# Down products and their way back to the tokens from one set of four PSUM banks

## The chip, the cores and the metric

The kernel runs on one core of a Trainium2 chip. The metric is the device time of one execution in microseconds (us). The kernel before took 1285.71 us, the median of three runs (1284.75 to 1287.04). One more execution was profiled; it took 1283.96 us, of which 1282.1 us lie between the first and the last instruction (the span).

Engines: TensorE (PE, with its weight loads as PEld) multiplies into PSUM, which has eight banks of 512 float32 for each of 128 partitions. VectorE (DVE) and ScalarE (ACT) read PSUM; GpSimd (POOL) works on SBUF alone; SyncE (SP) issues the loads of weights.

## The reference

Two layers, each an attention mixer and a mixture of experts, over 512 tokens of width 1024 in float32. The change lies in the mixture of experts: each token goes to two of 32 experts, each an MLP with a hidden width of 256.

```python
def hierarchical_moe(h, ...):
    ...                      # comb: each token's weight for its 2 of 32 experts, else 0
    y = jnp.zeros_like(hf)
    for g in range(N_GROUPS):
        a = jnp.einsum('nd,edf->nef', hf, w_gate[g])
        u = jnp.einsum('nd,edf->nef', hf, w_up[g])
        y = y + jnp.einsum('nef,efd->nd', jax.nn.silu(a) * u * comb[:, g, :, None], w_down[g])
    return y.reshape(B, S, D)

def reference(...):
    for l in range(DEPTH):
        ...
        x = x + gate_m * hybrid_mixer(h, ...)
        h = rms_norm(x, norm_ffn[l]) * (1.0 + scale_f) + shift_f
        x = x + gate_f * hierarchical_moe(h, ...)
    return x
```

## The kernel before

Each expert gets 64 slots for tokens. The expert stage (`moe`) goes through the experts in pairs, in 16 iterations a layer, so that the two experts of a pair fill the 128 partitions. One iteration `i` has these parts, in TensorE's order:

1. `down(i-1)` (lines 1062 to 1090): two tiles `d`, one for each half `q` of the 1024 output columns, 8 matmuls each. VectorE scales each with the slot weights and the gate (L1082, `o`), ScalarE and GpSimd split that into `ohi` and `olo` (L1087, L1088).
2. `hidden(i)` (lines 1035 to 1051): 32 matmuls into one tile `gu`; then the silu on ScalarE (L1049) and the product on VectorE (L1050) give `hs`.
3. The combine of pair `i-1`, from iteration 1 to 14: eight units, one for each of four token tiles `tt` and two halves `q`. A unit (`combine`, lines 1112 to 1118) is two matmuls with a 0/1 matrix `oT` that brings the rows of the slots back to their tokens, into a tile `y`; then `add` (L1095) on VectorE adds the tile to the residual stream `x`. Behind every second unit stands a pair of transposes `g` that gather rows for a later iteration (L1022), whose results VectorE and ScalarE copy out as `gT` (L1028, L1030). Behind the sixth unit stands the turn of `hs` (L1057), which ScalarE copies out as `hT` (L1059): the input of the next `down`.

Iteration 14 has nothing left to gather; iteration 15 has no combine, and `combine_last` (lines 1120 to 1140) does pairs 14 and 15 together, its first five units in five banks at once.

PSUM tiles come from `bank(name, tag, bufs)` (line 61). Tiles with one tag share `bufs` banks; a new tile waits until a bank of its tag has been read out. In the expert stage the tags are `d` (2), `y` (2), `g` (2), `gu` (1) and `misc` (1), all eight banks. `pm` (line 76) keeps the matmuls of the stage in the order in which they are written; the transposes are kept too. The instructions of VectorE and ScalarE around them are ordered when the program is built.

Weights come by DMA from SyncE's queue: 2 MB of gate and up weights (`wgu`, five tiles) and 1 MB of down weights (`wd`, four tiles) for each expert. Experts `2i+5` and `2i+6` are loaded into the tiles that `hidden(i)` frees, experts `2i+4` and `2i+5` of the down weights into those that `down(i)` frees. The gathered rows come by indirect DMA from GpSimd (L1003).

Of the kernel before, what the change touches and what calls it, by code (L numbers as in the profile page):

```python
# [29 lines left out]
def hybrid_decoder_kernel(ctx, tc, x, c, w_ada, b_ada, norm_mix, norm_ffn, w_in, w_gk2, b_gk, q_gain,  # L30
# [30 lines left out]
    def bank(name, tag, bufs, shape=None):  # L61
        return psum[1].tile(shape or [P, 512], F, name=name, tag=tag, bufs=bufs)
# [10 lines left out]
    def mm(o, a, b, start, stop):  # L73
        T.matmul(o, a, b, start=start, stop=stop, skip_group_check=True)  # L74

    def pm(o, a, b, start, stop):

        tc.keep_in_program_order(T.matmul(o, a, b, start=start, stop=stop, skip_group_check=True))  # L78

    def keep_warm(b, n):  # L80

        ps = bank("warm", "y", 2)
        for _ in range(n):
            pm(ps[:, 0:b.shape[-1]], ident, b, True, True)

# [799 lines left out]
    def moe(l, xt, ss, pool):  # L885
# [79 lines left out]
        for k, ix in ((0, i1), (1, i2)):  # L965
# [5 lines left out]
        V.tensor_tensor(exn.rearrange("p (t k) e -> p t (k e)", k=2), ex.rearrange("p t k e -> p t (k e)"),  # L971
                        tok[:, :, None].to_broadcast([P, NT, 2 * NE]), op=OP.mult)
        keep_warm(lo.rearrange("p t e -> p (t e)"), 10)

        rk = misc("rk", [P, NT + 1, NE])
        for tt in range(NT + 1):
            for t2 in range(min(tt + 1, NT)):
                pm(rk[:, tt], after_b if t2 == tt else ones_b, both[:, t2], tt == 0, t2 == min(tt, NT - 1))
        keep_warm(lo.rearrange("p t e -> p (t e)"), 6)
        pos = t3(2, "pos")  # L980
        tmp = pool.tile([P, NT, 2, NE], F, name="tmp")
# [80 lines left out]
        def down(hT, ws, i=None):  # L1062

            n = len(ws)
            r = slice(0, 64 * n)
            parts, last = [], None
            if i == NE // 2 - 1:

                last = wgu([P, 2, 2, 512], R, name="last")
            for q in range(2):  # L1070
                pd = bank("d", "d", 2)
                for j in range(2):
                    for e in range(n):
                        pm(pd[64 * e:64 * e + 64], hT[:, j, 64 * e:64 * e + 64],
                           ws[e][:, D * j + 512 * q:D * j + 512 * q + 512], j == 0, j == 1)
                o = ot([P, 512], name="o")
                gate = gates[l, 5][r, 512 * q:512 * q + 512]
                if i is None:
                    V.tensor_tensor(o[r], pd[r], gate, op=OP.mult)
                    parts.append(o)  # L1080
                else:
                    V.scalar_tensor_tensor(o, pd, cws[:, i:i + 1], gate, op0=OP.mult, op1=OP.mult)  # L1082
                    if last is not None:
                        hi, lo = last[:, q, 0], last[:, q, 1]
                    else:
                        hi, lo = ohl([P, 512], R, name="ohi"), ohl([P, 512], R, name="olo")
                    A.activation(hi, o, AF.Copy)  # L1087
                    (G if last is None else V).tensor_tensor(lo, o, hi.bitcast(F), op=OP.subtract)  # L1088
                    parts.append((hi, lo))
            return parts  # L1090

        def add(tt, q, ps, last):

            xc = xt[tt // 2][:, tt % 2, 512 * q:512 * q + 512]
            V.tensor_tensor(xc, ps, xc, op=OP.add)  # L1095
            if last:
                if l < L - 1:
                    square(ss, xt, tt, q)
                else:
                    SY.dma_start(out[0, P * tt:P * tt + P, 512 * q:512 * q + 512], xc)  # L1100
# [11 lines left out]
        def combine(u, oT, parts):  # L1112

            tt, q = units[u]
            ps = bank("y", "y", 2)
            for j in range(2):
                pm(ps, oT[:, P * tt:P * tt + P], parts[q][j], j == 0, j == 1)
            add(tt, q, ps, False)

        def combine_last(pairs):  # L1120

            order = [units[u] for u in (0, 2, 4, 6, 1, 3, 5, 7)]
            tags = [("y", 2), ("y", 2), ("g", 2), ("g", 2), ("gu", 1), ("misc", 1), ("d", 2), ("d", 2)]
            ps = {}

            def unit(n, u):
                tt, q = order[u]
                if n == 0:
                    ps[u] = bank("y", *tags[u])
                oT, parts = pairs[n]  # L1130
                for j in range(2):
                    pm(ps[u], oT[:, P * tt:P * tt + P], parts[q][j], n == 0 and j == 0, n == 1 and j == 1)
                if n:
                    add(tt, q, ps[u], True)

            for u in range(5):
                unit(0, u)
            yield
            for n, u in ((0, 5), (0, 6), (1, 0), (1, 1), (0, 7), (1, 2), (1, 3), (1, 4), (1, 5), (1, 6), (1, 7)):
                unit(n, u)  # L1140
# [18 lines left out]
        def add_rows(wT, o, n):  # L1159
            for tt in range(NT):  # L1160
                for q in range(2):
                    ps = bank("y", "y", 2)
                    mm(ps, wT[0:n, P * tt:P * tt + P], o[q][0:n], True, True)
                    add(tt, q, ps, True)

# [45 lines left out]
        def by_slot(values, name):  # L1211

            lst = misc(name, [P, NE])
            for i in range(NT * 2):
                pm(lst, ohp[i // NT][:, i % NT].rearrange("p a s -> p (a s)"), values[:, i], i == 0, i == NT * 2 - 1)
            return lst.rearrange("p (i a) -> p i a", a=2)
# [3 lines left out]
        for a in range(2):  # L1220
            numbered(nv[64 * a:64 * a + 64, :, a], idx[64 * a:64 * a + 64])
        keep_warm(lo.rearrange("p t e -> p (t e)"), 14)
        fetched = [fetch(idx[:, i:i + 1]) for i in range(4)]

# [23 lines left out]
        def weights_by_slot():  # L1248

            lv = by_slot(exw, "lst")  # L1250
            V.tensor_copy(cws[0:64], lv[0:64, :, 0])
            V.tensor_copy(cws[64:128], lv[64:128, :, 1])
            for k in range(2):
                ps = bank("slots", "y", 2)
                dg = ot([P, NT, P], name="dg")
                V.tensor_tensor(dg, ident[:, None, :].to_broadcast([P, NT, P]),
                                slot[:, :, k:k + 1].to_broadcast([P, NT, P]), op=OP.mult)
                for tt in range(NT):
                    pm(ps[:, P * tt:P * tt + P], n1.bitcast(F), dg[:, tt], tt == 0, True)
                A.copy(slots_row[:, k], ps)  # L1260
# [5 lines left out]
        for i in range(NE // 2):  # L1266
            while not {(0, 2 * i), (0, 2 * i + 1)} <= set(loaded):
                load_weights(1)
            if i % 2 == 0:
                now = gT  # L1270
                if i < NE // 2 - 2:
                    gT, rest = gather(fetched[i + 2:i + 4])
                    fetched += [fetch(idx[:, j:j + 1]) for j in range(i + 4, min(i + 6, NE // 2))]

            if i:
                part = places(i - 1), down(hT, [loaded.pop((1, e)) for e in (2 * i - 2, 2 * i - 1)], i - 1)
            *_, hs = hidden(now, P * (i % 2), [loaded.pop((0, e)) for e in (2 * i, 2 * i + 1)])
            load_weights(4)
            if i == 1:
                overflow_lists()  # L1280
            if i == NE // 2 - 1:
                break

            if i == 0:
                weights_by_slot()
            for u in range(4):
                for v in range(2):
                    if i:
                        combine(2 * u + v, *part)
                next(rest, None)  # L1290
                if u == 2:
                    hT = turn(hs)
        last = []
        end = combine_last([part, last])
        next(end)
        last += places(i), down(turn(hs), [loaded.pop((1, e)) for e in (2 * i, 2 * i + 1)], i)

        n_x = nc.values_load(xcnt[0:1, 0:1], min_val=0, max_val=NX)
# [93 lines left out]
```

## Time and profile before

| what | value |
|---|---|
| median of three runs | 1285.71 us (1284.75 to 1287.04) |
| profiled execution | 1283.96 us, span 1282.1 us |
| TensorE, matmul | 1172.3 us busy, 91% of the span |
| VectorE | 797.0 us, 62% |
| ScalarE | 462.7 us, 36% |
| DMA | 312.28 MB, mean 244 GB/s |
| expert stage, ten iterations of layer 1 | 167.29 us |

How to read it: a busy share is a mean over stages with different limits, so the expert stage has to be read by itself, one iteration in order of time. Times in such rows are microseconds from the span's start. Matmuls overlap, so the step from the start of one to the start of the next tells more than a duration. A number in brackets at a row's end is the idle time of the engine before it and what ended that.

### The profile page before, as it was taken

Reading aid. Unit: us, or ns where it says so; the run is one execution under the profiler, and the core shown is the slowest. Engines: PE = TensorE matmul, PEld = TensorE weight load, DVE = VectorE, ACT = ScalarE, POOL = GpSimd, SP = SyncE. Lnnn points to the kernel's source line nnn. Section 1 sums busy time; section 2 is a strip of 40 time slices with the busy share of each in tenths; the row PEclk is TensorE's granted clock in tenths of the full one; section 3 lists DMA queues with packets and bytes.
Section 4 is the critical chain, followed back from the end, with each engine's and each line's share of the span. In section 5 each row is a group of like instructions: output and inputs, shape, how many; then the busy total and the mean of one; then the engine's idle time right before and its main releaser. Section 6 shows DMA issues by size and latency. Waiting matters only on the chain. (4 is left out here: it accounts for less than half of the span.)

```text
span 1282.1 us, 16510 instructions
## 1 busy us (share of the span) xinstructions
PE 1172.3 (91%) x5935; PEld 739.7 (58%) x5935; DVE 797.0 (62%) x1484; ACT 462.7 (36%) x922; POOL 307.0 (24%) x330
## 2 busy tenths in 40 slices
PE   4989978977998999999988999899998899999996
PEld 2677746655885444444447877667787444444443
DVE  3488969796544555555546988877655355555553
ACT  3366635553251111111124775554535111111111
POOL 2122232244212222221103212434421222112110
PEclk9989989998979999999998999999998999999999
DMA  8454675751485999999805547763158699999961
GB/s 282 149 178 129 205 188 161 233 160 55 186 342 174 390 394 392 392 392 376 325 1 175 161 127 227 169 172 129 50 217 325 219 385 399 399 392 386 387 253 67
DMA packets 106285, 312.28 MB, mean 244 GB/s; under 512 B 13176, under 2 KB 50284, under 8 KB 81624
## 3 DMA queue, kind: packets, MB, share of 16 engines
q1 hardware_dynamic: 96920, 289.62, 62.6%
q0 software_dynamic: 9280, 21.57, 4.9%
q8 instruction: 48, 0.79, 0.3%
q14 instruction: 37, 0.30, 0.1%
HBM read 311.10 MB, written 8.43 MB: 249 GB/s over the span
## 5 line engine op out<-in xcount | busy, mean ns | idle before, releaser
L74 PE MATMUL proj<-whl,hh 128*128 128x512 f32 (+2 forms) x768 | 220.6, 370 | 7.4 <-ACT whl L95 6.2
L78 PE MATMUL gu<-wgu,gT 128*64 128x512 f32 x1024 | 225.8, 593 | 0.0
L1095 DVE TENSOR_TENSOR x<-y,x 128x512 f32<-128x512 f32 x240 | 153.9, 684 | 14.1 <-PE y L78 14.1
L78 PEld LDWEIGHTS gu<-wgu,gT 128*64 128x64 f32 x1024 | 73.5, 137 | 146.1 <-issue 146.1
L74 PEld LDWEIGHTS proj<-whl,hh 128*128 128x128 f32 x768 | 135.5, 191 | 36.1 <-issue 7.7
L1088 POOL TENSOR_TENSOR olo<-o,ohi 128x512 fp32r<-128x512 f32 x60 | 76.4, 1274 | 301.8 <-ACT ohi L1087 301.8
L96 POOL TENSOR_TENSOR whl<-raw,whl 128x512 fp32r<-128x512 f32 (+2 forms) x80 | 90.0, 1128 | 238.3 <-ACT whl L95 184.4
L1050 DVE TENSOR_TENSOR hs<-hs,gu 128x256 f32<-128x256 f32 x32 | 13.5, 421 | 204.4 <-ACT hs L1049 204.4
L74 PE MATMUL proj<-whl,hl 128*128 128x512 f32 (+2 forms) x384 | 139.0, 363 | 0.1
L255 DVE SCALAR_TENSOR_TENSOR row<-wada,ct,row 128x512 f32<-128x512 f32 x140 | 119.9, 856 | 16.8 <-DMA wada<-in_w_ada_dram 15.6
L78 PE MATMUL y<-ohi,oT 128*128 128x512 f32 x240 | 116.1, 484 | 6.9 <-DVE x L1095 6.9
L78 PE MATMUL d<-wd,hT 128*64 128x512 f32 x512 | 116.9, 598 | 1.4 <-ACT hT L1059 1.4
L1028 ACT ACTIVATE gT<-g,mod 128x256 f32<-128x256 f32 x64 | 35.9, 565 | 177.3 <-DVE gT L1030 177.3
L78 PE MATMUL y<-olo,oT 128*128 128x512 f32 x240 | 94.6, 394 | 0.0
L95 ACT ACTIVATE whl<-raw 128x512 fp32r<-128x512 f32 (+2 forms) x128 | 66.2, 524 | 68.3 <-PE proj L74 36.6
L78 PEld LDWEIGHTS y<-ohi,oT 128*128 128x128 f32 x240 | 44.8, 186 | 74.8 <-DVE x L1095 45.4
L74 PEld LDWEIGHTS proj<-whl,hl 128*128 128x128 f32 x384 | 72.6, 189 | 13.4 <-issue 3.0
L1049 ACT ACTIVATE hs<-gu 128x256 f32<-128x256 f32 x32 | 12.3, 384 | 169.9 <-PE gu L78 169.9
L78 PEld LDWEIGHTS d<-wd,hT 128*64 128x64 f32 x512 | 33.9, 136 | 62.2 <-issue 59.9
L1082 DVE SCALAR_TENSOR_TENSOR o<-d,cws,gate_f 128x512 f32<-128x512 f32 x64 | 47.7, 748 | 34.9 <-PE d L78 34.9
L1087 ACT ACTIVATE ohi<-o 128x512 fp32r<-128x512 f32 x60 | 37.8, 629 | 78.9 <-DVE o L1082 78.8
L1003 POOL DMA_INDIRECT rows<-xg,idx x32 | 32.8, 1025 | 126.0 <-PE g L1022 108.9
(339 smaller groups left out, 2041.6 us busy)
## 6 DMA issues: line engine op xcount, KB each, us to landing
wgu<-in_w_gate_dram SPq DMA_DIRECT2D x64, 1024.0 KB, 7.7
wgu<-in_w_up_dram SPq DMA_DIRECT2D x64, 1024.0 KB, 10.3
wd<-in_w_down_dram SPq DMA_DIRECT2D x64, 1024.0 KB, 8.8
wada<-in_w_ada_dram SPq DMA_DIRECT2D x96, 512.0 KB, 4.3
raw<-in_w_in_dram SPq DMA_DIRECT2D x80, 256.0 KB, 3.6
raw<-in_w_out_dram SPq DMA_DIRECT2D x16, 512.0 KB, 3.7
raw<-in_w_in_dram SPq DMA_DIRECT2D x32, 128.0 KB, 2.9
xg<-xn POOLq DMA_DIRECT2D x8, 512.0 KB, 2.9
```

Of the source, the lines that this page charges most:

```text
L74: T.matmul(o, a, b, start=start, stop=stop, skip_group_check=True)
L78: tc.keep_in_program_order(T.matmul(o, a, b, start=start, stop=stop, skip_group_check=True))
L95: A.activation(hi, src, AF.Copy)
L96: eng.tensor_tensor(lo, src, hi.bitcast(F), op=OP.subtract)
L255: V.scalar_tensor_tensor(row, ws[k], ct1[:, k:k + 1], row, op0=OP.mult, op1=OP.add)
L1003: G.indirect_dma_start(r, None, xg[:, :], bass.IndirectOffsetOnAxis(ap=idx, axis=0), bounds_check=S - 1, oob_is_err=False)
L1028: A.activation(o, src, AF.Identity, scale=m, bias=b)
L1050: V.tensor_tensor(hs[r], hs[r], gu[r, 256:512], op=OP.mult)
L1082: V.scalar_tensor_tensor(o, pd, cws[:, i:i + 1], gate, op0=OP.mult, op1=OP.mult)
L1087: A.activation(hi, o, AF.Copy)
L1088: (G if last is None else V).tensor_tensor(lo, o, hi.bitcast(F), op=OP.subtract)
L1095: V.tensor_tensor(xc, ps, xc, op=OP.add)
```

## The change

The tags `d` and `y`, with two banks each, become one tag `dy` with four. Every tile that had one of them is changed: the down products, the units of the combine, those of the last combine and of the loop for overflow rows, the warm-up products and the slot numbers. Nothing is computed in another way, and no instruction is moved in the program.

```diff
@@ keep_warm
-        ps = bank("warm", "y", 2)
+        ps = bank("warm", "dy", 4)
@@ down
-                pd = bank("d", "d", 2)
+                pd = bank("d", "dy", 4)
@@ combine
-            ps = bank("y", "y", 2)
+            ps = bank("y", "dy", 4)
@@ combine_last
-            tags = [("y", 2), ("y", 2), ("g", 2), ("g", 2), ("gu", 1), ("misc", 1), ("d", 2), ("d", 2)]
+            tags = [("dy", 4), ("dy", 4), ("g", 2), ("g", 2), ("gu", 1), ("misc", 1), ("dy", 4), ("dy", 4)]
@@ add_rows
-                    ps = bank("y", "y", 2)
+                    ps = bank("y", "dy", 4)
@@ weights_by_slot
-                ps = bank("slots", "y", 2)
+                ps = bank("slots", "dy", 4)
```

## Rows read from the trace of the kernel before

**Rows 1.** The page, part 1: busy time, share of the span, instructions of TensorE.
```profile
PE 1172.3 (91%) x5935; PEld 739.7 (58%) x5935; DVE 797.0 (62%) x1484; ACT 462.7 (36%) x922; POOL 307.0 (24%) x330
```

**Rows 2.** Windows, ten iterations: length, busy time (instructions) by engine, clock, DMA share, GB/s.
```profile
1036.44:1203.73 167.29, 165.12 (x743) 72.19 (x740) 88.54 (x150) 31.47 (x60) 33.62 (x29) 1.00 0.99 395
```

**Rows 3.** TensorE's waits: total us, times, longest.
```profile
PE y L78 <- DVE x L1095: 6.9, 30, 0.4
```

**Rows 4.** One iteration's combine on TensorE in order of time: start, us, instruction.
```profile
1093.43 0.50 PE L78 MATMUL y<-ohi,oT 128*128 128x512 f32 x1
1093.77 0.39 PE L78 MATMUL y<-olo,oT 128*128 128x512 f32 x1
...
1094.46 0.38 PE L1022 MATMUL g<-ident,rows 128*128 128x128 f32 x2
...
1095.06 0.50 PE L78 MATMUL y<-ohi,oT 128*128 128x512 f32 x1 [0.22 <-DVE x L1095]
...
1097.74 0.38 PE L1022 MATMUL g<-ident,rows 128*128 128x128 f32 x2
...
1097.96 0.40 PE L1057 MATMUL hsT<-ident,hs 128*128 128x128 f32 x2
...
1098.22 0.51 PE L78 MATMUL y<-ohi,oT 128*128 128x512 f32 x1
...
1099.39 0.38 PE L1022 MATMUL g<-ident,rows 128*128 128x128 f32 x2
1099.70 0.65 PE L78 MATMUL d<-wd,hT 128*64 128x512 f32 x2
```

**Rows 5.** TensorE in iteration 14 and the last combine, in order of time.
```profile
1244.01 0.50 PE L78 MATMUL y<-ohi,oT 128*128 128x512 f32 x1
...
1249.95 3.65 PE L78 MATMUL d<-wd,hT 128*64 128x512 f32 x16
1253.44 7.04 PE L78 MATMUL gu<-wgu,gT 128*64 128x512 f32 x32
1260.40 0.51 PE L78 MATMUL y<-ohi,oT 128*128 128x512 f32 x1
...
1262.82 0.39 PE L1057 MATMUL hsT<-ident,hs 128*128 128x128 f32 x2
1263.68 3.65 PE L78 MATMUL d<-wd,hT 128*64 128x512 f32 x16 [0.46 <-ACT hT L1059]
```

**Rows 6.** VectorE in the stretch of rows 4, and its first adds in iteration 14.
```profile
1094.33 1.28 DVE L1095 TENSOR_TENSOR x<-y,x 128x512 f32<-128x512 f32 x2
...
1095.83 1.29 DVE L1095 TENSOR_TENSOR x<-y,x 128x512 f32<-128x512 f32 x2 [0.23 <-PE y L78]
...
1097.04 0.53 DVE L1030 TENSOR_SCALAR gT<-g,mod 128x256 f32<-128x256 f32 x1
...
1097.49 1.28 DVE L1095 TENSOR_TENSOR x<-y,x 128x512 f32<-128x512 f32 x2
...
1244.91 1.28 DVE L1095 TENSOR_TENSOR x<-y,x 128x512 f32<-128x512 f32 x2
```

**Rows 7.** ScalarE in the stretch of rows 4.
```profile
1097.61 0.56 ACT L1028 ACTIVATE gT<-g,mod 128x256 f32<-128x256 f32 x1 [3.65 <-DVE gT L1030]
...
1098.40 0.37 ACT L1059 COPY hT<-hsT 128x256 f32<-128x256 f32 x1 [0.23 <-PE hsT L1057]
```

**Rows 8.** Line 78's separate wait instructions: count, ns minimum, median, maximum.
```profile
L78 PEldq EVENT_SEMAPHORE  x103: 51/51/51, 386.8 to 1261.4; - x103
```

**Rows 9.** Last loads of layer 1, issue and landing: `wgu`, then `wd`.
```profile
1227.74 0.42 SPq L909 DMA_DIRECT2D wgu<-in_w_up_dram  x1
...
DMA to landing us min/median/max: 7.6/7.6/7.6
...
1237.24 0.81 SPq L905 DMA_DIRECT2D wd<-in_w_down_dram  x2
...
DMA to landing us min/median/max: 4.9/6.5/8.1
```

## The prediction

> **What bounds the kernel now.** I read the page's head first (TensorE is busy for 91% of the span [rows 1]), then the table of windows, the list of waits, and last one iteration in order of time on each engine. In the expert stage TensorE runs an exact cycle: ten iterations take 167.29 us, 16.73 us each, at a granted clock of 1.00, the 2.4 GHz level [rows 2]. The list of waits has no wait of TensorE for expert weights; it has the wait that the change is about, products `y` for the add `x` on VectorE [rows 3]. 6.9 us in 30 waits looks like nothing, but that view counts only matmuls that found the array idle, so I measured the stretch itself: from the first `y` of an iteration (1093.43) to the first `d` (1099.70) it is 6.27 us [rows 4]. Fourteen iterations of a layer (1 to 14) have this stretch, the last of them without the gather's transposes; layer 0 has the same fourteen.
>
> **What the stretch costs when nothing waits.** Its pieces stand in the same rows. The first matmul of a unit after a break takes 0.34 us to the next (1093.43 to 1093.77), each further one 0.23 (three, up to the transposes at 1094.46). Two units in a row take 0.34 + 3 x 0.23 = 1.03 us. A pair of gather transposes takes 0.22 (1097.74 to 1097.96), the turn of `hs` 0.26 (to 1098.22), and from the last pair to the first `d` go 0.31 (1099.39 to 1099.70) [rows 4]. That several units stream at this pace when each has a bank of its own is shown once a layer: the last combine sends five units into five banks from 1260.40 to 1262.82, 2.42 us, and 0.34 + 9 x 0.23 is 2.41 [rows 5].
>
> **The change part by part.** The instructions stay the same, and TensorE's order is written out; only the bank that each `d` and `y` tile gets is another. Removed: units 2 to 7 of a combine no longer wait for the add two units back. Now the third unit starts at 1095.06 where the transposes before it are through at 94.46 + 0.22 = 94.68 (I leave out the leading 10 from here): 0.38 lost in one wait [rows 4]. With four banks the stretch runs from 93.43 for 4 x 1.03 + 3 x 0.22 + 0.26 to the last pair, at 98.47, and `d` comes at 98.78 in place of 99.70: 0.92 us less. Of this 3 x 0.11 are weight loads that a wait between two units leaves in the open (0.34 in place of 0.23 for the fourth, sixth and eighth unit); the rest are the waits.
>
> This holds only if VectorE frees the banks in time. Its adds start at 94.33 and follow each other at 0.64 (1.28 for two); the gather's `gT` takes 0.45 of its queue (97.04 to 97.49) [rows 6]. Without idle time the adds of units 0 to 3 end at 94.97, 95.61, 96.25, 96.89, then comes `gT`, and those of units 4 to 7 end at 97.98, 98.62, 99.26, 99.90. A waiting matmul starts 0.09 after the end (94.97 and 95.06). TensorE gets to units 4, 5, 6, 7 at 95.93, 96.50, 97.44, 98.01 and needs the banks of units 0 to 3, free 0.8 to 1.1 us earlier each. Units 2 and 3 take the banks of the last down products, read out long before.
>
> Added: the down products now stand in line behind adds. The first `d` (98.78) needs the bank of unit 4, free at 98.07, 0.71 to spare; the second, half of 3.49 later (1249.95 to 1253.44 for both [rows 5]), that of unit 5, free at 98.71. Behind a late `d` stand the 32 `gu` of the next iteration on TensorE, and VectorE and ScalarE wait for those. While this cover lasts the cost is nothing. VectorE ends its adds at 99.90, when TensorE is in `d`: this is the work that moves off the path, and nothing is late next, as the two `o` that VectorE owes to `d` still come after it. The other input of `d` is `hT`, copied on ScalarE behind its half of `gT`, which waits for VectorE's half. These are now at 97.61 (0.56 long) and 98.40 (0.37) [rows 7]. After the change VectorE's `gT` ends at 96.89 + 0.53 = 97.42, ScalarE's at 98.02 and the copy at 98.42, so `d` could start by 98.45: 0.33 to spare.
>
> The first `d` may carry one wait more (add, copy and weights in place of copy and weights). No row of before shows that one; the nearest is TensorE's separate wait instruction, 51 ns [rows 8]. Bounds 0 and 0.05 us for each of 28, 1.4 us in all; I take 0, as the add is over before TensorE arrives, and a wait that is added can't gain.
>
> Iteration 14 has no transposes: now 1244.01 to 1249.95, 5.94 us [rows 5]. Unhindered: 0.34 + 11 x 0.23 for six units, 0.26 for the turn, 0.34 + 3 x 0.23 for two more and 0.09 up to `d` (0.31 less the 0.22 of a pair), 4.25 us. The adds, 0.64 apart from 1244.91 [rows 6], just keep ahead. 1.69 us less.
>
> The other users (warm-up products, slot numbers, the last combine) run where banks are free, and the last combine has as many banks as it had: 0, with 0.5 us either way as bounds, from the 0.46 us wait there [rows 5]. The loop for overflow rows runs no iteration in this trace.
>
> **Sum.** For each layer 13 x 0.92 + 1.69 = 13.65 us; for two, 27.3 us. The profiled execution took 1283.96 us (span 1282.1), so its time would become 1256.7. The three timed runs have a median of 1285.71, 1.75 above it; against these the sum gives 1258.4, and that is my forecast.
>
> **Do the weights keep up?** DMA is 0.99 busy at 395 GB/s [rows 2], the strongest objection: iterations of 15.81 us ask for 395 x 16.73 / 15.81 = 418 GB/s. But loads run ahead of their use. Suppose DMA can go no faster than now, so that every load lands when it lands today. The last gate and up weights of a layer are issued by 1227.74, land 7.6 us later, at 1235.3, and are used at 1253.44: 18.1 us ahead. The last down weights land by about 1237.6 + 8.1 = 1245.7 and are used at 1263.68, 18.0 ahead [rows 5, 9]. A layer saves 13.65 us up to there, so even then TensorE waits for nothing, with 4 us left.
> The Trainium skill, DMA: Bandwidth & Descriptors, section Bandwidth, gives 425 GB/s for a 16 MB load with the pair's other core idle, and says that the HBM side binds at about 358 GB/s. The trace disagrees with the second figure: 395 over ten iterations. As an estimate from that page, the 6.61 MB of an iteration (395 GB/s in 16.73 us) take 15.6 us at 425, a little less than the new cycle, and 18.5 us at 358, more than today's.
>
> **Rivals.**
> DMA sets the cycle from the start (the lead is used up by something that I don't see): an iteration then can't fall below 0.99 x 16.73 = 16.56 us, and the gain is 2 x (13 x 0.17 + 1.69) = 7.8 us: 1277.9. For it speaks the share of 0.99, against it the 18 us of lead. Chance 0.05.
>
> ScalarE's queue. If VectorE's order puts `gT` behind the add of unit 4, the copy of `hT`, and so `d`, comes 0.64 - 0.33 = 0.31 late and an iteration gains 0.61: 1266.5. Behind unit 5 too, 0.95 late, and these thirteen gain nothing. For it: with more banks those adds are ready earlier, so they can come first. Against it: VectorE's order in before is the program's, `gT` behind the fourth add [rows 6]. Such a partial gain, 1262 to 1275: chance 0.13.
>
> Slower: the bank that `d` gets is the one freed last. Before, `d` had two banks of its own and never waited for an add. Given that of unit 7, it starts after the whole chain of adds, at 99.99, 0.29 later than now; in iteration 14 at 1244.91 + 8 x 0.64 + 0.09 = 1250.12, 0.17 later. 2 x (13 x 0.29 + 0.17) = 7.9 us more: 1293.6. It decides between unit 6 (99.35, still 0.35 gained) and unit 7. For it: only one common set makes this wait possible at all [rows 4, 6]. Against it: a tile that takes the bank freed first gets unit 4's. Chance 0.06, two thirds of it beyond 0.2%.
> The Trainium skill, PSUM — Partial Sum Buffer, section PSUM bank collisions raise a hardware error, says that two engines have to be kept off one bank at the same time, with semaphores for each bank. By that rule the wait of `d` for the add in its bank can't be left out; the trace agrees for `y`, whose matmul starts 0.09 us after the add that frees its bank.
>
> The sets are not shared as the change says (each user settles on two banks): no gain, 1285.7, chance 0.03.
>
> More than forecast: the weight loads that stay in the open in four units of each stretch vanish too: 4 x 0.11 x 26 = 11.4 us more, 1247.0. Chance 0.09.
>
> **How the numbers follow.** Forecast 0.64 (1255 to 1261), partial gain 0.13, more 0.09, slower 0.06, DMA 0.05, none 0.03. From 1249 to 1271 lie the forecast, part of "more" and most of the partial gains, some 0.8. A measurement of this kernel can tell about 0.2%, 2.6 us, from no change. Faster by more: 0.64 + 0.13 + 0.09 + 0.05 less 0.01 of near cases, 0.90. Within it: 0.05. Slower: 0.05.
>
> **What would show it.** Right: `y` for `x` gone from the list of waits, or nearly; cycles of 15.8 us at clock 1.00; 5.35 us from first `y` to first `d`; the last adds of an iteration beside `d`; DMA near 418 GB/s, and no wait of `gu` or `d` for weights. Wrong: a wait of `d` for `x` or `hT`; one of `gu` for `wgu`; `gT` behind more than four adds; a lower clock, now that TensorE hardly pauses.

## The result and the profile after

The changed kernel took 1246.35 us, the median of four runs (1242.96 to 1253.52), beside 1286.38 us for the kernel before (four runs now): a ratio of 0.9706, 95% interval 0.9675 to 0.9737. Six more runs have a median of 1249.87 and, beside 17 more of the kernel before, gave 0.9699 (0.9658 to 0.9739). It is faster, as forecast, but by about 37 to 40 us where 27.3 were forecast, and 1246.35 lies below the range of 1249 to 1271. The profiled execution took 1248.04 us (span 1246.3), against 1283.96 before.

The answer to [rows 1], and the windows of ten iterations that answer to [rows 2] (length, busy time by engine with instructions, clock, DMA share, GB/s), from the changed kernel:

```profile
PE 1139.3 (91%) x5935; PEld 740.5 (59%) x5935; DVE 791.1 (63%) x1484; ACT 459.7 (37%) x922; POOL 308.8 (25%) x330
...
1033.21:1187.74 154.53, 154.53 (x743) 73.21 (x740) 85.75 (x150) 30.46 (x60) 33.45 (x28) 1.00 1.01 420
```

The same 5935 matmuls, and the same share of the span; the busy share alone says nothing of the change. Ten iterations now take 154.53 us, 15.45 each in place of 16.73, and TensorE is busy for all of it at the same granted clock of 1.00, the 2.4 GHz level. DMA moves 420 GB/s where it moved 395. In the list of TensorE's waits the line of [rows 3] is gone; of the expert stage this is left, as it was before:

```profile
PE d L78 <- ACT hT L1059: 1.4, 4, 0.5
```

One combine on TensorE in order of time, the stretch that answers to [rows 4]:

```profile
1070.91 0.50 PE L78 MATMUL y<-ohi,oT 128*128 128x512 f32 x1
...
1071.25 0.39 PE L78 MATMUL y<-olo,oT 128*128 128x512 f32 x1
...
1071.95 0.38 PE L1022 MATMUL g<-ident,rows 128*128 128x128 f32 x2
1072.06 0.19 PEld L78 LDWEIGHTS y<-ohi,oT 128*128 128x128 f32 x1
1072.08 0.48 PE L78 MATMUL y<-ohi,oT 128*128 128x512 f32 x1
...
1072.40 0.40 PE L78 MATMUL y<-olo,oT 128*128 128x512 f32 x1
...
1074.23 0.38 PE L1022 MATMUL g<-ident,rows 128*128 128x128 f32 x2
...
1074.45 0.40 PE L1057 MATMUL hsT<-ident,hs 128*128 128x128 f32 x2
...
1074.60 0.47 PE L78 MATMUL y<-ohi,oT 128*128 128x512 f32 x1
...
1075.61 0.38 PE L1022 MATMUL g<-ident,rows 128*128 128x128 f32 x2
...
1075.92 3.65 PE L78 MATMUL d<-wd,hT 128*64 128x512 f32 x16
```

From the first `y` to the first `d` it is 5.01 us (6.27 before, 5.35 forecast), and no row of a matmul carries a wait. VectorE and ScalarE in this stretch, beside [rows 6] and [rows 7]:

```profile
1071.81 2.47 DVE L1095 TENSOR_TENSOR x<-y,x 128x512 f32<-128x512 f32 x4
...
1074.21 0.53 DVE L1030 TENSOR_SCALAR gT<-g,mod 128x256 f32<-128x256 f32 x1
...
1074.66 2.47 DVE L1095 TENSOR_TENSOR x<-y,x 128x512 f32<-128x512 f32 x4
...
1074.88 0.37 ACT L1059 COPY hT<-hsT 128x256 f32<-128x256 f32 x1 [3.44 <-PE hsT L1057]
...
1075.15 0.57 ACT L1028 ACTIVATE gT<-g,mod 128x256 f32<-128x256 f32 x1
...
1078.16 0.74 DVE L1082 SCALAR_TENSOR_TENSOR o<-d,cws,gate_f 128x512 f32<-128x512 f32 x1
```

The adds run in two blocks of four without a pause, and the last of them ends at 1077.13, 1.2 us after `d` has begun: that is the work which has left the path. On ScalarE the copy of `hT` now comes ahead of `gT`.

**Where the time went.** From the second to the sixteenth gate and up product of a layer (the starts of the first `gu` matmul of each iteration) it was 233.93 and 233.89 us in the two layers of the profiled execution; now it is 215.47 and 215.48. That is 36.9 us, inside the interval of the ratio (0.0263 to 0.0325 of 1286.38, 33.8 to 41.8 us). The rest of an execution isn't the same twice: to the first `gu` of layer 0 it took 400.24 us before and 390.33 after, from the last of layer 0 to the first of layer 1 353.50 and 362.75. Of what the change touches, only the warm-up products, the slot numbers and the last combine lie outside the stage, and from the last `gu` of layer 1 to the end it is 28.66 us before and 28.67 after. Windows of one such stretch, the end of the second mixer, in the kernel before and in the changed one:

```profile
958.00:981.00 23.00, 21.63 (x144) 19.05 (x143) 10.98 (x30) 12.25 (x25) 1.88 (x2) 0.99 0.99 402
```

```profile
940.00:962.00 22.00, 21.65 (x121) 20.01 (x119) 6.84 (x14) 9.02 (x21) 1.29 (x1) 0.75 0.93 375
```

The granted clock has a mean of 0.99 in one and 0.75 in the other, a mixture of both levels. So two single executions can differ by 10 us outside the expert stage, and below the cycle of the expert stage is the measure, and the time only its confirmation.

### The profile page after: what moved, and what is told of

Read it like the earlier page. It is cut to its first block, busy times and chain, and to the rows that moved or that the text cites. A ratio compares the mean times of both kernels' runs of the same rounds, so it can differ in the third digit from the quotient of the medians.

```text
span 1246.3 us, 16510 instructions
## 1 busy us (share of the span) xinstructions
PE 1139.3 (91%) x5935; PEld 740.5 (59%) x5935; DVE 791.1 (63%) x1484; ACT 459.7 (37%) x922; POOL 308.8 (25%) x330
## 5 line engine op out<-in xcount | busy, mean ns | idle before, releaser
L1095 DVE TENSOR_TENSOR x<-y,x 128x512 f32<-128x512 f32 x240 | 148.2, 679 | 0.9 <-PE y L78 0.9
L78 PE MATMUL y<-ohi,oT 128*128 128x512 f32 x240 | 104.5, 435 | 0.0
## 6 DMA issues: line engine op xcount, KB each, us to landing
wgu<-in_w_gate_dram SPq DMA_DIRECT2D x64, 1024.0 KB, 10.2
```

## The experiments

Theory: products waited for the add that holds their bank; a common set of four frees them because the two users need banks at different times, and what is left is TensorE's own work. Rivals: the set does something of its own; the weights; ScalarE's order; the bank that `d` gets. Each ratio is to runs of the kernel before that were taken with it (medians 1286.38 us for the changed kernel, 1288.40 from after_again to last_freed, 1281.19 from split_3_1 to apart).

| kernel | cycle, us | 2nd to 16th `gu`, us | ratio to before, 95% interval |
|---|---|---|---|
| before | 16.73 | 233.9 | |
| changed | 15.45 | 215.5 | 0.9706 (0.9675 to 0.9737) |
| after_again | 15.45 | 215.5 | 0.9699 (0.9658 to 0.9739) |
| short_adds | 15.5 | 216.4 | 0.9741 (0.9696 to 0.9785) |
| three_banks | 15.81 | 220.7 | 0.9813 (0.9766 to 0.9860) |
| last_freed | 16.74 | 233.9 | 0.9989 (0.9962 to 1.0016) |
| split_3_1 | 16.95 | 236.8 | 1.0132 (1.0072 to 1.0191) |
| no_up | 15.45 | 215.5 | 0.9726 (0.9669 to 0.9783) |
| gu6 | 13.73, then 14.1 to 16.2 | 199.8 | 0.9465 (0.9410 to 0.9520) |
| apart | 15.49 | 215.9 | 0.9674 (0.9629 to 0.9719) |
| hT_behind | 15.45 | 215.5 | one execution |

**The changed kernel again (after_again).** No edit.

> The changed kernel again, five more rounds. The four runs so far lie between 1243 and 1253.5 us. Theory: the spread comes from the mixers, where the granted clock falls after idle stretches, and not from the expert stage. Then the profile shows a cycle of 15.45 us in the expert stage as before, while the time from the end of layer 0's stage to the start of layer 1's moves by several us. Rival: the spread comes from weights that land too late in the expert stage, now that DMA moves 419 GB/s; then the cycle itself varies, and TensorE waits for wgu or wd.

The executions lay between 1242.4 and 1253.7 us, but the stage took 215.47 and 215.46 us in this profile too, and TensorE waited for no weights. From the last `gu` of layer 0 to the first of layer 1 it took 361.06 us, to the first `gu` of layer 0 395.39 (362.75 and 390.33 in the first profile). In the profiled executions the differences lie outside the expert stage; the ones at the ends of the spread were not profiled, and that the clock makes it is not shown. The kernel before has such a spread as well: 1281.5 to 1294.6 in 17 runs beside these.

**Short adds in the old banks (short_adds).** An edit to the kernel before:

```diff
-            V.tensor_tensor(xc, ps, xc, op=OP.add)
+            w = slice(0, 512 if last else 64)
+            V.tensor_tensor(xc[:, w], ps[:, w], xc[:, w], op=OP.add)
```

> The kernel before with its two sets of two banks, but each add of a combine (other than the last ones) takes 64 of the 512 columns; the other columns of these sums are left out. If the change paid only because products no longer wait for adds, this kernel has the changed kernel's cycle, 15.45 us (15.4 to 15.6), with the old banks, and is some 36 us faster than before. It is also what the stretch costs when nothing waits: 5.0 us from first y to first d. My working from the rows of before gave 5.35 and so a cycle of 15.81; if that was right about the pieces, this kernel shows 15.8. Rival, that the common set does something of its own: the cycle stays above 16.2.

With the old two sets of two the cycle falls to 15.5. First `y` and first `d` of one iteration:

```profile
1043.95 0.50 PE L78 MATMUL y<-ohi,oT 128*128 128x512 f32 x1
...
1049.03 3.65 PE L78 MATMUL d<-wd,hT 128*64 128x512 f32 x16
```

5.08 us. So 1.23 of the 1.28 us that a cycle gains by the change are the wait for adds, and the pieces of my sum were too dear whatever the banks.

**Three common banks (three_banks).** `("dy", 4)` becomes `("dy", 3)` throughout; one bank stays empty.

> The common set has three banks in place of four, one bank is unused. By the adds' times in the changed kernel (four in 2.47 us, then gT, then four more), only the eighth unit comes before its bank is free, by about 0.2 us, and a weight load of 0.1 us is then in the open: a cycle of 15.7 to 15.85, 25 to 29 us faster than before. If instead each bank counts alike, the cycle is halfway, 16.1. If the fourth bank is of no use, 15.45.

15.81, within the expectation. The step that makes it, the seventh unit's second matmul, the eighth unit's two:

```profile
1113.55 0.39 PE L78 MATMUL y<-olo,oT 128*128 128x512 f32 x1
...
1113.93 0.50 PE L78 MATMUL y<-ohi,oT 128*128 128x512 f32 x1
1114.27 0.40 PE L78 MATMUL y<-olo,oT 128*128 128x512 f32 x1
```

0.38 from the seventh unit to the eighth and 0.34 within it, where 0.23 each is the pace: 0.26 of the 0.36 us in one place. The eighth unit alone was expected to wait, but the weight loads of the fourth and the sixth wait for adds too, which makes 0.07 more.

```profile
1111.08 0.19 PEld L78 LDWEIGHTS y<-ohi,oT 128*128 128x128 f32 x1 [0.19 <-DVE x L1095]
...
1112.28 0.19 PEld L78 LDWEIGHTS y<-ohi,oT 128*128 128x128 f32 x1 [0.21 <-DVE x L1095]
```

Three common banks bring 0.92 us of the 1.28, the fourth the rest. That 0.92 and 15.81 are also what the prediction had for four banks is chance.

**The bank freed last (last_freed).** Four banks by name; the down products take those of units 7 and 6. Two of the places are shown, against the changed kernel; the other users of `dy` get a bank by name too.

```diff
-                pd = bank("d", "dy", 4)
+                pd = bank("d", f"b{3 - q}", 1)
@@ combine
-            ps = bank("y", "dy", 4)
+            ps = bank("y", f"b{u % 4}", 1)
```

> Four banks as in the changed kernel, but each by name: unit u of a combine takes bank u mod 4, and the first down product takes the bank of unit 7, freed last, the second that of unit 6. This is the slower rival of the prediction. d then starts about 0.08 us after the last add, which ends 6.2 us after the first y (77.13 against 70.91 in the changed kernel's trace): d 1.25 us later, a cycle of 16.7, and within 0.5% of the kernel before. If the down products don't wait in that way (the semaphores follow the tag, not the bank, or VectorE's order adapts), the cycle is 15.5 to 16.

The whole gain is gone. VectorE's adds, then TensorE's last transposes and `d`:

```profile
1102.32 2.47 DVE L1095 TENSOR_TENSOR x<-y,x 128x512 f32<-128x512 f32 x4
...
1103.29 0.38 PE L1022 MATMUL g<-ident,rows 128*128 128x128 f32 x2
1104.89 3.65 PE L78 MATMUL d<-wd,hT 128*64 128x512 f32 x16 [1.22 <-issue]
```

The last add ends at 1104.79; `d` starts 0.10 us later, 1.60 after the transposes in place of 0.31. The row names "issue" as releaser. A separate wait instruction of TensorE ahead of `d` says more; it waits for a semaphore of VectorE and one of a load. In [rows 8] all of these take 51 ns, here it takes 2.83 us, from 1102.01 to 1104.83, 0.04 behind the last add (count, ns minimum, median, maximum, start):

```profile
L78 PEldq EVENT_SEMAPHORE  x1: 2829/2829/2829, 1102.0 to 1102.0; - x1
```

The same four banks are worth 37 us or nothing, by which of them the next user gets.

**The same four banks as three and one (split_3_1).** An edit to the kernel before (two of its places; the other users of `y` and `d` likewise):

```diff
-            ps = bank("y", "y", 2)
+            ps = bank("y", "y", 3)
-                pd = bank("d", "d", 2)
+                pd = bank("d", "d", 1)
```

> The same four banks, but split into three for y and one for d. If what counts is that the two users need their banks at different times, this split is worse than the common set: the eighth unit waits as with three common banks (a cycle of 15.81 was measured there), and the second down product waits until VectorE has read the first one, which it does only after its adds. In the changed kernel's trace VectorE starts on the first o at 78.16 and is through at 78.90, where the second d would start at 77.7: 1.2 to 1.6 us more. A cycle of 16.8 to 17.3, and so no gain on before or a small loss. If three banks for y were what paid, it is 15.8 to 16.

16.95, and 1.3% slower than before. The two down products and VectorE's reading of the first:

```profile
1112.02 1.94 PE L78 MATMUL d<-wd,hT 128*64 128x512 f32 x8
...
1114.07 0.75 DVE L1082 SCALAR_TENSOR_TENSOR o<-d,cws,gate_f 128x512 f32<-128x512 f32 x1
...
1114.88 1.94 PE L78 MATMUL d<-wd,hT 128*64 128x512 f32 x8 [0.92 <-DVE o L1082]
```

The second product stands until VectorE has come through its adds to the first `o`. The cycles make only 5.8 of the 17 us that this kernel loses. Some 12 lie in the first iterations, which the table leaves out: from the first to the second `gu` it takes 21.8 and 22.1 us in the two layers (15.7 and 16.2 before), with the same wait, longer:

```profile
1028.41 3.52 PE L78 MATMUL d<-wd,hT 128*64 128x512 f32 x8 [3.71 <-DVE o L1082]
```

With two banks each it is `y` that waits, with three and one it is `d` above all; the common set lets both through.

**No up weights (no_up).** The gate weights stand in for the up weights.

```diff
-                for h, w in enumerate((w_gate, w_up)):
+                for h, w in enumerate((w_gate,)):
-                       ws[i][:, :, 256 * k:256 * k + 256], k == 0, k == KT - 1)
+                       ws[i][:, 0:1, 256 * k:256 * k + 256].to_broadcast([P, 2, 256]), k == 0, k == KT - 1)
```

> The changed kernel without the loads of the up weights: the gate weights are used in their place, by the same number of matmuls, so that part of the result is another and a third of the expert weights is not moved. If TensorE's own work sets the changed cycle, it stays 15.45 with DMA some 0.65 busy. If transfers slow TensorE or the others down (the rate rose to 419 GB/s at a share of 1.01), the cycle falls below 15.4. If the spread of the executions came from late weights, it shrinks below 3 us; if it comes from the mixers' clock, it stays some 10 us.

The cycle is 15.45 to the hundredth, with this load on DMA (windows of 200 us of layer 1's stage, columns as above):

```profile
1001.00:1201.00 200.00, 200.00 (x962) 94.85 (x960) 118.36 (x204) 39.48 (x78) 43.16 (x36) 1.00 0.75 281
```

So the transfers at 420 GB/s cost the changed kernel nothing. The spread was 4.5 us in four runs, between the two expectations; it decides nothing by itself.

**Fewer gate and up products (gu6).** The changed kernel with this edit:

```diff
-            for k in range(KT):
+            for k in (0, 1, 2, 4, 5, 7):
```

> The changed kernel with six of the eight matmul pairs of each gate and up product; the sums lack two eighths of their terms. This takes 8 of 32 matmuls, 1.72 us, from TensorE in each iteration and leaves the transfers as they are: how much more could TensorE gain before the weights set the cycle? If the weights always keep up, the cycle is 13.73 in all iterations. If DMA is at its limit at 419 GB/s, the 6.5 MB of an iteration take 15.6 us: the first six or seven iterations run at 13.73 on the lead of the loads, some 12 us, and the later ones at 15.4 to 15.8 with TensorE waiting for wgu. Then from the second to the sixteenth gate and up product it takes 203 to 209 us (215.5 in the changed kernel, 191.4 without any wait).

Both parts show: eight cycles of 13.73, then, in layer 0, 14.06, 15.56, 16.18, 14.91, 14.93 and 14.05. The stretch took 199.5 and 200.0 us, less than the 203 to 209 expected, as the lead lasted for eight iterations and not for six or seven. TensorE's waits in layer 1, and the landing of the `wgu` loads from issue:

```profile
PE gu L78 <- DMA wgu<-in_w_up_dram: 2.1, 5, 1.4
...
DMA to landing us min/median/max: 11.3/19.8/21.8
```

These are waits that the changed kernel doesn't have. From 1082 to 1158.8 us, the cycles with waits in layer 1, DMA moved 421 GB/s. The changed kernel's 420 is almost as much: its cycle of 15.45 us moves 6.49 MB, which would take 15.4 us at 421, so it stands close to its second limit. TensorE can gain about 1.7 us more of a cycle for half the stage, and little after that.

**Transposes between units (apart).** The one attempt to beat the changed kernel.

```diff
-            for u in range(4):
-                for v in range(2):
-                    if i:
-                        combine(2 * u + v, *part)
-                next(rest, None)
-                if u == 2:
+            for u in range(8):
+                if i:
+                    combine(u, *part)
+                if u in (1, 3, 5, 6):
+                    next(rest, None)
+                if u == 4:
                     hT = turn(hs)
```

> The changed kernel with the gather's transposes and the turn each between two units: the fourth pair before unit 7 in place of behind it, the turn behind the fifth unit in place of next to the third pair. By the pieces measured in the changed kernel (a pair that a unit follows 0.13 us, a pair that the turn follows 0.22, the turn 0.15, a pair that d follows 0.31, d behind a unit 0.10 more than its matmul's 0.23) the stretch takes 4 x 0.13 + 0.15 + 0.10 = 0.77 in place of 3 x 0.13 less 0.13 for the one before the turn, plus 0.22 + 0.15 + 0.31, that is 0.94: a cycle of 15.28 (15.2 to 15.35), 4 to 5 us less than the changed kernel in both layers, if the adds and the weights still keep up. If these gaps belong to the change between kinds of matmul and not to the place, the cycle stays 15.4 to 15.5.

A miss: 15.49, 0.03 more than the changed kernel, in place of 15.28. The time of the runs (0.9674) can't be told from the changed kernel's. The end of the stretch:

```profile
1072.41 0.38 PE L1022 MATMUL g<-ident,rows 128*128 128x128 f32 x2
1072.55 0.48 PE L78 MATMUL y<-ohi,oT 128*128 128x512 f32 x1
1072.87 0.39 PE L78 MATMUL y<-olo,oT 128*128 128x512 f32 x1
1073.19 3.65 PE L78 MATMUL d<-wd,hT 128*64 128x512 f32 x16
```

A pair is followed by a unit after 0.14 us, but that unit's first matmul then takes 0.32 in place of 0.23. The two belong together: a pair costs about 0.22 wherever it stands, and I had counted the first half alone.

**ScalarE's order of before (hT_behind).** The changed kernel with this edit:

```diff
-            A.copy(hT, ps[:, 0:256].rearrange("p (j s) -> p j s", j=2))
+            tc.keep_in_program_order(A.copy(hT, ps[:, 0:256].rearrange("p (j s) -> p j s", j=2)))
```

> The changed kernel, with ScalarE's copy of hT kept behind its half of gT, as it stood in the kernel before (in the changed kernel the copy comes first, at 1074.88, and gT at 1075.15). This is the queue of the prediction's ScalarE rival. VectorE's gT ends at 1074.74 there, so ScalarE's would end at 75.35 and the copy at 75.75, 0.17 before the first d at 75.92. If that is all, the cycle stays 15.45 (up to 15.5) and the new order of ScalarE has no part in the gain. If the copy gets later than that, the cycle is 15.6 to 16.

The cycle stays 15.45; the copy ends 0.32 us before `d`:

```profile
1080.12 0.56 ACT L1028 ACTIVATE gT<-g,mod 128x256 f32<-128x256 f32 x1 [3.34 <-DVE gT L1030]
1080.58 0.36 ACT L1059 COPY hT<-hsT 128x256 f32<-128x256 f32 x1
...
1081.26 3.65 PE L78 MATMUL d<-wd,hT 128*64 128x512 f32 x16
```

The new order on ScalarE has no part in the gain. (This execution took 1253.4 us beside 1279.76 of before: 26 us apart with the same 36.9 us in the stage, which shows what a single pair of executions is worth.)

## Why the prediction was wrong

**The bound and the mechanism: right.** TensorE's cycle was set by waits of `y` for adds; they are gone, VectorE's last adds run beside `d`, and the cycle is TensorE's own work. short_adds shows it without the change, and no_up shows that the transfers have no part in the cycle that is left.

**The term that failed: the cost of the stretch when nothing waits.** I made it 5.35 us from [rows 4]; it measures 5.01. Each iteration of the thirteen gains 1.28 and not 0.92 (16.73 to 15.45), and 26 x 0.36 is 9.4 us; with 0.2 from iteration 14 the forecast is 9.6 us short in the stage. The other 2.4 of the 12.0 us between 1258.4 and 1246.35 lie outside it, in the spread. Two steps were wrong: one counts a weight load twice, the other was read from a row that was itself waiting.

First, a unit behind a pair of transposes. I added the 0.22 from a pair to the turn and the 0.34 of a unit behind a break, 0.56. The trace of after has 0.13 (1071.95 to 1072.08) and 0.32 (to 1072.40), 0.45. The unit's weight load begins at 1072.06, 0.11 after the transposes do, and from there it is the same 0.34 to the second matmul. The 0.22 held a weight load already, the turn's, which begins 0.11 ahead of its matmul at 1097.96. A row of the kernel before shows it:

```profile
1097.85 0.32 PEld L1057 LDWEIGHTS hsT<-ident,hs 128*128 128x128 f32 x2
```

Taking both prices counted such a load twice. This happens at units 2 and 4.

Second, the turn. The 0.26 to 1098.22 was no price of the turn: the `y` there waited for the add of the fifth unit, the first of the two from 1097.49; half of their 1.28 later is 1098.13, and my own 0.09 more is 1098.22 [rows 4, 6]. Unhindered it is 0.15, and 0.32 behind it: 0.47 in place of 0.60. 0.11 + 0.11 + 0.13 is 0.35, and the stretch was 0.34 too long (5.35 to 5.01). [rows 5] could not have warned me, as the five units there follow each other with no transposes between; the row of 1097.85 could.

**Iteration 14: nearly right.** 1209.99 to 1214.12 in the changed kernel, 4.13 us, where 4.25 was worked out: 1.81 gained in place of 1.69.

**The sum** with the measured steps is 2 x (13 x 1.28 + 1.81) = 36.9, which is what the stage shows.

**The rival "more than forecast"** had almost the right time (1247.0), by luck: its reason is another, and 2.4 us of what was measured lie outside the stage. The loads in the open don't vanish: in apart a unit's first matmul behind a pair still takes 0.32. They had been counted twice. I gave it 0.09 and ended the range at 1249, inside it; a doubt of 0.11 us in a piece that occurs four times in each of 26 stretches was worth a wider lower end.

**VectorE frees the banks in time: right**, with somewhat less to spare than worked out. Adds that don't wait follow each other at 0.60 (four in 2.47 us with the last one's end), not at 0.64, which as half of a pair's 1.28 [rows 6] has that end in it. But TensorE comes sooner too. The fifth unit starts at 1073.23, and the add of the first, whose bank it takes, ends at 1072.49. With 0.05 us from an add's end to the end of a wait for it, the banks of the fifth to the eighth unit are free 0.6 to 0.9 us ahead, where 0.8 to 1.1 was worked out. three_banks shows how much room that is: with one bank less the fourth, sixth and eighth unit wait.

**The slower rival: the mechanism is shown, with the size a little off.** Handing `d` the bank of unit 7 puts it 0.10 us behind the last add. I gave 7.9 us more than before; it came out at the time of before (16.74 against 16.73 a cycle), as the adds were faster. It decided between no gain and 37 us. In the changed kernel `d` gets the bank that is free first: the wait instruction ahead of it ends at 1075.38, 0.05 behind the add of the fifth unit (1075.33) and 0.54 ahead of `d`.

```profile
L78 PEldq EVENT_SEMAPHORE  x1: 1036/1036/1036, 1074.3 to 1074.3; - x1
```

(Two thirds of the 0.06 are 0.04, and not the 0.05 that stands for slower at the end of the prediction.)

**ScalarE's queue: off the path.** Its order did change, in the other direction (copy first), and hT_behind shows that neither order matters.

**The weights: right, with a margin.** The last gate and up loads of layer 1, issue and landing, beside [rows 9]:

```profile
1195.02 0.42 SPq L909 DMA_DIRECT2D wgu<-in_w_up_dram  x1
...
DMA to landing us min/median/max: 11.1/11.1/11.1
```

They land at 1206.1 and are used at 1217.61: 11.5 us ahead, 18.1 before. The worst case that I allowed, landing at the times of before, would have left 18.1 - 18.4 us, nothing at all, now that the stage is 18.4 us shorter; it was needed only in part, since DMA was not at its limit. 0.99 busy at 395 GB/s became 1.01 at 420. The figure of 425 GB/s from the Trainium skill, DMA: Bandwidth & Descriptors, section Bandwidth, is within 2% of that; the 358 GB/s of the same section is not what binds here. How near the limit is, gu6 shows.

**The wait that `d` might carry: it is there, and costs nothing.** It is the wait shown with the slower rival, 1.04 us long where the one before `d` took 51 ns [rows 8], and it is over before `d` could start: from the last transposes to `d` it is 0.31 us, as before.

## What to carry to other kernels

Two users of PSUM that need it in turn did better here with one set than with two halves of it, because the bank that the next user got was one freed early; the same four banks gave 16.95, 16.73, 16.74 or 15.45 us a cycle by how they were dealt out. Before a stretch is priced without its waits, ask of each step whether the row it is read from was waiting itself, and whether two steps count the same weight load. Where a transfer looks saturated, the lead between landing and use says whether it can hurt; the busy share doesn't.

## What was not expected of the hardware

DMA at a share of 0.99 had 6% left: 395 GB/s before, 420 at 1.01 in the changed kernel, with loads issued earlier and more of them queued (the median landing of the gate loads went from 7.7 to 10.2 us on the page).

A pair of 128x128 transposes between matmuls of 512 columns costs TensorE 0.22 us in each place that was tried: 0.22 ahead of the turn, or 0.13 and 0.09 more in the next matmul ahead of a unit.

The same instructions gave mixers of different length from one execution to the next, with the granted clock at 0.75 in a stretch where it had been 0.99. What made the clock fall there was not looked into.
